# Weight low halves on GpSimd, row maxima scaled by a per-partition scalar

## The chip, the cores and the metric

The kernel runs on one core of a Trainium2 chip. The metric is the device time of one launch in microseconds (us). The engines are called by the profile's names: PE is TensorE (matmul), DVE is VectorE, ACT is ScalarE, POOL is GpSimd, and SP is SyncE, which here only issues DMAs. Each engine runs its own list of instructions in order and waits on semaphores for the others.

## The reference

Two blocks of two layers each, over 512 positions of width 1024, all in float32. The first block's layer projects x, runs four attentions (MLA, stick-breaking, Fox with forget gates, and one over a memory), gates each with a Silu, merges them with sigmoid gates, projects out and normalizes:

```python
    h = x @ w_in
    (c_q, c_kv, k_rope, sb_qkv, fox_qkv, fox_f, mem_q, gate_z, merge_r) = _split_last(h, IN_SPLITS)
    ...
    branches = (y_mla, y_sb, y_fox, y_mem)
    gate_z = gate_z.reshape(b, s, N_BRANCHES, BRANCH_WIDTH)
    merge_g = jax.nn.sigmoid(merge_r @ w_merge_up).reshape(b, s, N_BRANCHES, D_MODEL)
    merged = jnp.zeros_like(x)
    for n in range(N_BRANCHES):
        yb = branches[n].reshape(b, s, BRANCH_WIDTH) * jax.nn.silu(gate_z[:, :, n])
        merged = merged + merge_g[:, :, n] * (yb @ w_branch[n])
    out = merged @ w_out
    return _layer_norm(DEEPNORM_ALPHA * x + out, ln_g, ln_b)
```

The second block's layer has the same outline with other attentions: dense (a), a window with a sink (b), a neighbourhood with a table of biases (c), and differential attention (d), in which the softmax of one half of the channels is subtracted, times a factor, from that of the other half. Its branches are gated by Silu too, projected out, added to x, and RMS-normalized.

## The kernel before

Every float32 matmul is done as three products of halves. A number a is split into a high half ah, which PE's fast float32 format holds exactly, and a low half al = a − ah; `mm3` (L324) then adds ah·bh (L328), ah·bl (L329) and al·bh (L330) in PSUM. `split` (L317) makes the halves in two instructions: ACT copies the source into the high half, rounding it (L319), and DVE subtracts it from the source (L322). Activations are split so, from PSUM (tiles th and tl, zth and ztl), and weights too.

The weights lie in HBM as 184 units of 128 x 1024 numbers, 512 KB each, in the order of use. `w_prefetch` (L356) takes them in this order: a DMA on SP's queue brings a unit into one of three raw buffers (L376), and `split` makes wh and wl of it, in one of three pairs of buffers. The 28 units of the output projections (wo, wo2) go into an own pair of tiles (wout), and four units of the memory projection (m) are split in two halves each. `w_get` (L389) hands a unit out and lets the prefetch run up to three units ahead. A raw buffer is free again when the subtraction has read it.

`proj_fm` multiplies a unit with the layer's input. `softmax` (L515) takes the row maxima of a score tile on DVE, negated (L525 with a mask, L528 without), scales them where the scores carry a factor (L532: 64 instructions on 128 x 1 numbers, 32 in the MLA attention and 32 in the dense one), and gives them to ACT as the bias of Exp (L534). Transposes of p on PE follow (L552, tile T, split into th and tl), and the product with V (L564, L565, tile O). `silu` (L603) applies Silu to the gates on ACT (L608) and then loads the table of functions with Exp and Ln again (L611); ACT needs a table load wherever the function changes between the two sets. At the differential attention the scores are made at L1395 and combined at L1403.

`merge` (L1085) runs over eight output tiles m. A unit mu serves two of them, a unit wb one. For each branch, projmu gives the sigmoid gate, projwb the branch's product, and DVE adds them up (L1106, L1110). `w_out` (L1116) then takes all wo units, and for each quarter of the rows loads the residual y (L1126) on SP's queue and adds the product to it (L1134).

Attentions, gates and projections of a layer are written as generators, which two strings, ORDER1 and ORDER2, weave together. The final place of each instruction in its engine's list is set by a list scheduler, from its own estimates of durations, so an instruction that moves to another engine can shift others around it on all engines. POOL has almost nothing to do: it sets constants, the Fox rows (L1056, L1057) and the tiles V (L443) to fixed values.

Of the kernel before, what the change touches and what calls it, by code (L numbers as in the profile page):

```python
# [14 lines left out]
ALU = mybir.AluOpType  # L15
# [273 lines left out]
def cols(i, n=128):  # L289
    return slice(n * i, n * i + n)  # L290
# [11 lines left out]
WP = 3  # L302
# [8 lines left out]
class Build:  # L311
# [2 lines left out]
        self.layers = range(n_layers) if isinstance(n_layers, int) else n_layers  # L314


    def split(self, h, l, src, eng=None):  # L317
        if eng is None:
            self.nc.scalar.copy(h, src)  # L319
        else:  # L320
            eng.tensor_copy(h, src)
        self.nc.vector.tensor_tensor(l, src, h, ALU.subtract)  # L322

    def mm3(self, ps, pairs):  # L324

# [31 lines left out]
    def w_prefetch(self, upto):  # L357
        nc = self.nc
        while self.w_done < min(upto, len(UNITS)):
            i = self.w_done  # L360
            key = UNITS[i]
            wd = WIDTH.get(key[0], 1024)
            if key[0] in ("wo", "wo2"):
                if self.wout is None:
                    break
                parts = [tuple(w[:, key[2]] for w in self.wout)]
            elif key[0] == "m":
                if self.stp is None:
                    break
                parts = [(self.st("mh"), self.st("ml")) for _ in range(2)]  # L370
            else:
                parts = [tuple(self.wp.tile([128, 1024], F32R, tag=t, name=t)[:, :wd] for t in ("wh", "wl"))]
            raw = self.rawp.tile([128, 1024], F32, tag="raw", name="raw")
            n = 2 if i == 0 else 1
            for c in (cols(j, wd // n) for j in range(n)):
                nc.sync.dma_start(raw[:, c], self.ins["w"][i, :, c])  # L376
                if key[0] != "m":
                    self.split(*(t[:, c] for t in parts[0]), raw[:, c])
            if key[0] == "m":
                for j, (h, l) in enumerate(parts):  # L380
                    self.split(h, l, raw[:, cols(j, 512)])
            self.w_ready[key] = parts if key[0] == "m" else parts[0]
            self.w_done += 1
# [132 lines left out]
    def softmax(self, i, s, w, sm, mask=None, sscale=None, p=None, nm=None, top=BIG):  # L516


        nc = self.nc
        if p is None:  # L520
            p = self.pp.tile([128, w], F32, tag=f"p{i}", name="p", bufs=self.pb[i])
        nm = self.small(1, "nm") if nm is None else nm
        src, sc = s, 1.0
        if mask is not None:
            nc.vector.tensor_tensor_reduce(p[:, :w], s, mask, -1.0, top, ALU.add, ALU.min, nm)  # L525
            src, sc = p[:, :w], -1.0
        else:
            nc.vector.tensor_reduce(nm, s, AX.X, ALU.max, negate=True)  # L528
        if sscale is not None:
            sc = sscale[1 if mask is not None else 0]  # L530
            nm2 = self.small(1, "nm2")
            nc.vector.tensor_tensor(nm2, nm, sscale[0], ALU.mult)  # L532
            nm = nm2
        nc.scalar.activation(p[:, :w], src, AF.Exp, bias=nm, scale=sc, accum_out=sm)  # L534
        return p
# [945 lines left out]
```

## Time and profile before

| quantity | value |
|---|---|
| time, median of 3 runs | 1417.88 us (1415.82 to 1418.38) |
| the profiled execution | 1419.11 us, its span 1417.3 us |
| mean granted PE clock, as a share of full speed | 0.986 |
| PE busy | 1363.2 us, 7112 matmuls |
| DVE busy | 999.9 us, 2077 instructions |
| ACT busy | 832.3 us, 1672 instructions |
| POOL busy | 4.3 us, 12 instructions |

The span is what the trace covers, from the first instruction to the last. Busy times of engines overlap, so they don't add up to it. The chain is the sequence of work that ended last, followed back from the end: at each step to what released it, or to the instruction before it on its engine. The granted clock is what the chip allowed PE to run at in a stretch, 1.00 being full speed.

### The profile page before, as it was taken

How to read it: one execution, taken by the hardware profiler on the slowest of the kernel's cores; microseconds unless marked ns; L12 is line 12 of the kernel's file. 1: busy time of each engine (PE TensorE's matmuls, PEld its weight loads, DVE VectorE, ACT ScalarE, POOL GpSimd, SP SyncE). 2: the span in 40 equal slices, each digit the busy share in tenths (PEclk: the TensorE clock that was granted, in tenths of full speed). 3: DMA queues.
4: the chain of work that ended last, by engine and by line, in shares of the span. 5: the costliest groups of instructions: out<-in, count | busy, mean ns of one | idle time of the engine just before them, and what ended most of it. 6: DMA issues, size and time to landing. Idle time of an engine off the chain costs nothing.

```text
span 1417.3 us, 20005 instructions
## 1 busy us (share of the span) xinstructions
PE 1363.2 (96%) x7112; PEld 1111.0 (78%) x7112; DVE 999.9 (71%) x2077; ACT 832.3 (59%) x1672; POOL 4.3 (0%) x12
## 2 busy tenths in 40 slices
PE   8999998999999999998999999999999999999998
PEld 7887786777789777877777788877777888877776
DVE  6666545898764776257989675887777575886785
ACT  5584547765413765476856243776866346667763
POOL 0000000000000000000000000000000000000000
PEclk9999999999999999999999999999999999999999
DMA  7534222213625424222135436323434265215241
GB/s 238 172 105 118 72 75 80 75 60 108 207 100 159 139 71 117 75 81 80 41 89 179 163 115 180 111 60 103 131 100 145 109 177 150 75 45 151 62 140 67
DMA packets 61266, 160.31 MB, mean 113 GB/s; under 512 B 11056, under 2 KB 11696, under 8 KB 61168
## 3 DMA queue, kind: packets, MB, share of 16 engines
q1 hardware_dynamic: 61168, 159.05, 37.8%
q8 instruction: 56, 0.92, 0.3%
q14 instruction: 42, 0.34, 0.1%
HBM read 117.92 MB, written 8.91 MB: 89 GB/s over the span
## 4 chain that ended last, share of the span: by engine, by line
PE 77%; ACT 8%; DVE 8%; DMA 4%; issue 2%; SPq 0%; DVEq 0%; ACTq 0%
PE proj L328 11%; PE proj L329 11%; PE proj L330 11%; PE T L552 3%; PE pso L328 3%; PE pso L329 3%; PE pso L330 3%; PE O L564 3%; PE O L565 2%; PE s L901 2%; PE projv L329 2%; PE projv L330 2%; PE projv L328 2%; PE projwb L329 2%; PE projwb L330 2%
## 5 line engine op out<-in xcount | busy, mean ns | idle before, releaser
L328 PE MATMUL proj<-zth,wh 128*128 128x512 f32 (+1 forms) x864 | 323.9, 375 | 9.5 <-ACT wh L319 5.8
L329 PE MATMUL proj<-ztl,wh 128*128 128x512 f32 (+1 forms) x864 | 323.4, 374 | 0.3
L330 PE MATMUL proj<-zth,wl 128*128 128x512 f32 (+1 forms) x864 | 322.9, 374 | 0.0
L322 DVE TENSOR_TENSOR wl<-raw,wh 128x1024 fp32r<-128x1024 f32 (+2 forms) x153 | 183.1, 1197 | 135.1 <-ACT wh L319 126.7
L319 ACT CAST wh<-raw 128x1024 fp32r<-128x1024 f32 (+2 forms) x153 | 157.6, 1030 | 170.4 <-PE proj L329 139.7
L328 PEld LDWEIGHTS proj<-zth,wh 128*128 128x128 f32 x864 | 164.1, 190 | 32.9 <-ACT wh L319 5.8
L330 PEld LDWEIGHTS proj<-zth,wl 128*128 128x128 f32 x864 | 164.2, 190 | 23.7 <-DVE wl L322 1.0
L329 PEld LDWEIGHTS proj<-ztl,wh 128*128 128x128 f32 x864 | 164.3, 190 | 22.8 <-DVE ztl L322 0.7
L322 DVE TENSOR_TENSOR tl<-T,th 128x512 fp32r<-128x512 f32 (+3 forms) x176 | 98.9, 576 | 28.3 <-ACT th L319 27.7
L552 PE MATMUL T<-ct,p 128*128 128x128 f32 x560 | 103.6, 279 | 9.9 <-ACT p L534 7.7
L319 ACT CAST th<-T 128x512 fp32r<-128x512 f32 (+3 forms) x176 | 85.5, 498 | 41.8 <-PE T L552 39.0
L552 PEld LDWEIGHTS T<-ct,p 128*128 128x128 f32 x560 | 71.1, 142 | 30.5 <-ACT p L534 11.3
L528 DVE TENSOR_REDUCE nm<-s 128x1 f32<-128x512 f32 (+1 forms) x128 | 77.5, 616 | 19.6 <-PE s L513 10.2
L534 ACT ACTIVATE p<-s,nm 128x512 f32<-128x512 f32 (+1 forms) x96 | 59.1, 619 | 17.3 <-DVE nm L528 16.7
L564 PE MATMUL O<-th,V 128*128 128x512 f32 (+3 forms) x176 | 62.4, 371 | 2.6 <-ACT th L319 2.2
L565 PE MATMUL O<-tl,V 128*128 128x512 f32 (+3 forms) x160 | 59.3, 376 | 5.0 <-DVE tl L322 4.8
L328 PE MATMUL pso<-wout,zth 128*128 128x512 f32 x128 | 51.7, 404 | 4.7 <-DVE y L1134 4.7
L328 PE MATMUL projv<-wh,zth 128*128 128x256 f32 (+1 forms) x192 | 55.0, 287 | 0.0
L330 PE MATMUL projv<-wh,ztl 128*128 128x256 f32 (+1 forms) x192 | 54.7, 285 | 0.0
L329 PE MATMUL projv<-wl,zth 128*128 128x256 f32 (+1 forms) x192 | 54.6, 284 | 0.0
L330 PE MATMUL projwb<-y,wl 128*128 128x512 f32 x128 | 51.6, 403 | 0.0
L328 PE MATMUL projwb<-y,wh 128*128 128x512 f32 x128 | 51.1, 399 | 0.2
(380 smaller groups left out, 2927.7 us busy)
## 6 DMA issues: line engine op xcount, KB each, us to landing
raw<-in_w_dram SPq DMA_DIRECT2D x173, 512.0 KB
xs<-y SPq DMA_DIRECT2D x12, 512.0 KB
ks<-hs SPq DMA_DIRECT2D x32, 128.0 KB
early<-xs SPq DMA_DIRECT2D x16, 256.0 KB
bias<-in_bias_dram SPq DMA_DIRECT2D x8, 448.0 KB
qs<-hs SPq DMA_DIRECT2D x24, 128.0 KB
qs<-ls SPq DMA_DIRECT2D x24, 128.0 KB
hs<-ls SPq DMA_DIRECT2D x24, 128.0 KB
```

The source lines that it names most:

```text
L319: self.nc.scalar.copy(h, src)
L322: self.nc.vector.tensor_tensor(l, src, h, ALU.subtract)
L328: self.nc.tensor.matmul(ps, ah, bh, start=i == 0, stop=False)
L329: self.nc.tensor.matmul(ps, ah, bl, start=False, stop=False)
L330: self.nc.tensor.matmul(ps, al, bh, start=False, stop=i == n - 1)
L528: nc.vector.tensor_reduce(nm, s, AX.X, ALU.max, negate=True)
L534: nc.scalar.activation(p[:, :w], src, AF.Exp, bias=nm, scale=sc, accum_out=sm)
L552: nc.tensor.transpose(T[:, cols(a)], P[i][:, c : c + 128], self.ident)
L564: nc.tensor.matmul(o[:, c], vsel(j), th[:, c], start=j == 0, stop=False)
L565: nc.tensor.matmul(o, vsel(j), tl[:, :w], start=False, stop=j == nk - 1)
L901: nc.tensor.matmul(z[:, c:w], m, x, start=False, stop=n == len(sums) - 1, skip_group_check=True)
```

## The change

`split` gets a parameter for the engine that does the subtraction. `w_prefetch` passes POOL for all units from the fourth on, except the four m units: 177 of 181 subtractions of weight halves other than those of the m units, 139 of 1024 columns, six of 876, two of 768, two of 384, and the 28 of wo and wo2. The scaling of the row maxima becomes a tensor_scalar whose scalar comes from a 128 x 1 tile.

```diff
-    def split(self, h, l, src, eng=None):
+    def split(self, h, l, src, eng=None, sub=None):
         if eng is None:
             self.nc.scalar.copy(h, src)
         else:
             eng.tensor_copy(h, src)
-        self.nc.vector.tensor_tensor(l, src, h, ALU.subtract)
+        (sub or self.nc.vector).tensor_tensor(l, src, h, ALU.subtract)
...
                 if key[0] != "m":
-                    self.split(*(t[:, c] for t in parts[0]), raw[:, c])
+                    self.split(*(t[:, c] for t in parts[0]), raw[:, c], sub=nc.gpsimd if i >= WP else None)
...
             nm2 = self.small(1, "nm2")
-            nc.vector.tensor_tensor(nm2, nm, sscale[0], ALU.mult)
+            nc.vector.tensor_scalar(nm2, nm, sscale[0], None, ALU.mult)
             nm = nm2
```

The scheduler places much else anew. ACT's list at the first group of Silus in layer 2, before (L534 is Exp; th, ot and V are copies out of PSUM):

```order
L608 ACT_TABLE_LOAD
L608 ACTIVATE z<-z 128x512
L319 CAST th<-T 128x512
L608 ACTIVATE z<-z 128x512
L319 CAST th<-T 128x512
L608 ACTIVATE z<-z 128x512 x2
L611 ACT_TABLE_LOAD
L592 COPY ot<-O 64x512
L534 ACTIVATE p_9115,s_9113<-s,nm 128x512
```

And the beginning of the same group after the change:

```order
L608 ACT_TABLE_LOAD
L608 ACTIVATE z<-z 128x512
L592 COPY ot<-O 64x512
L534 ACT_TABLE_LOAD
L534 ACTIVATE p,sums<-s,nm 128x512
L534 ACTIVATE p_9115,s_9113<-s,nm 128x512
L608 ACT_TABLE_LOAD
L608 ACTIVATE z<-z 128x512
L534 ACT_TABLE_LOAD
L534 ACTIVATE p,sums<-s,nm 128x512
L534 ACTIVATE p_9132,s_9130<-s,nm 128x512
L414 CAST V<-projv 128x4x64
```

The group of four Silus with two table loads has become one with nine loads up to its last, with Exps in between, and layer 3 has the same. The groups of layers 0 and 1 have five loads instead of seven each.

PE's list in a merge, at the turn from one mu unit (wh_2627, wl_2628) to the next (wh_3250, wl_3251), before; wh_3317 and wl_3318 are the wb unit that is fetched there:

```order
L329 MATMUL projwb_3373<-y_3206,wh_3244 128x512
L328 MATMUL projmu_3367<-mr_3240,wh_2627 128x512
L329 MATMUL projmu_3367<-mr_3241,wh_2627 128x512
L330 MATMUL projmu_3367<-mr_3240,wl_2628 128x512
L330 MATMUL projwb_3373<-y_3205,wl_3245 128x512
L328 MATMUL projwb_3402<-y_3177,wh_3317 128x512
L329 MATMUL projwb_3402<-y_3178,wh_3317 128x512
L328 MATMUL projmu_3396<-mr_3240,wh_3250 128x512
L329 MATMUL projmu_3396<-mr_3241,wh_3250 128x512
L330 MATMUL projmu_3396<-mr_3240,wl_3251 128x512
L330 MATMUL projwb_3402<-y_3177,wl_3318 128x512
```

After:

```order
L330 MATMUL projmu_3367<-mr_3240,wl_2628 128x512
L329 MATMUL projwb_3373<-y_3202,wh_3244 128x512
L330 MATMUL projwb_3373<-y_3201,wl_3245 128x512
L328 MATMUL projwb_3373<-y_3205,wh_3244 128x512
L329 MATMUL projwb_3373<-y_3206,wh_3244 128x512
L330 MATMUL projwb_3373<-y_3205,wl_3245 128x512
L328 MATMUL projmu_3396<-mr_3240,wh_3250 128x512
L329 MATMUL projmu_3396<-mr_3241,wh_3250 128x512
L330 MATMUL projmu_3396<-mr_3240,wl_3251 128x512
L328 MATMUL projwb_3402<-y_3177,wh_3317 128x512
L329 MATMUL projwb_3402<-y_3178,wh_3317 128x512
L330 MATMUL projwb_3402<-y_3177,wl_3318 128x512
```

Before, the high half's products of the new wb unit stand ahead of the new mu unit's; after, they stand behind them, directly ahead of the low half's. From the matmul that is the last to read the buffer which the wb unit takes over, to the one that reads its low half, there are ten matmuls before and twelve after.

## Rows read from the trace of the kernel before

**Rows 1.** The page: span, busy time by engine, chain by engine.

```profile
span 1417.3 us, 20005 instructions
...
PE 1363.2 (96%) x7112; PEld 1111.0 (78%) x7112; DVE 999.9 (71%) x2077; ACT 832.3 (59%) x1672; POOL 4.3 (0%) x12
...
PE 77%; ACT 8%; DVE 8%; DMA 4%; issue 2%; SPq 0%; DVEq 0%; ACTq 0%
```

**Rows 2.** Windows: stretch, us, busy PE, PEld, DVE, ACT, POOL, clock, DMA, GB/s.

```profile
200.00:250.00 50.00, 45.08 (x218) 35.76 (x217) 29.59 (x72) 34.96 (x67) 0.00 (x0) 0.93 0.26 72
875.00:925.00 50.00, 49.99 (x277) 41.80 (x276) 33.64 (x65) 32.71 (x65) 0.00 (x0) 1.00 0.45 126
899.90:917.90 18.00, 18.00 (x125) 16.16 (x124) 13.66 (x31) 15.60 (x32) 0.00 (x0) 1.00 0.27 76
```

**Rows 3.** DVE's groups by form, weight subtractions: busy us, mean ns, idle before.

```profile
L322 DVE TENSOR_TENSOR wl<-raw,wh 128x1024 fp32r<-128x1024 f32 x141 | 172.3, 1222 | 122.0 <-ACT wh L319 113.6 <-DMA bias<-in_bias_dram 2.4 <-PE s L512 2.0
...
L322 DVE TENSOR_TENSOR wout<-raw,wout 128x1024 fp32r<-128x1024 f32 x28 | 34.2, 1222 | 5.1 <-ACT wout L319 5.1
...
L322 DVE TENSOR_TENSOR wl<-raw,wh 128x876 fp32r<-128x876 f32 x6 | 6.4, 1071 | 12.8 <-ACT wh L319 12.8
```

**Rows 4.** Waits: who waits for whom, total us, times, longest.

```profile
DVE wl L322 <- ACT wh L319: 126.7, 61, 7.2
```

**Rows 5.** Chain that ended last, in order of time: start, us, piece.

```profile
60.77 0.59 DVE wl L322
...
249.75 1.08 DVE wl L322
250.83 0.73 DVE rw L748
...
345.52 1.23 DVE wout L322
...
346.77 3.61 DMA raw<-in_w_dram
...
1286.21 1.24 DVE wl L322
```

**Rows 6.** Timeline of POOL, a memset: start, us, instruction, idle before.

```profile
64.93 0.53 POOL L1056 MEMSET cqrows<- 128x512 f32 x1 [64.49 <-DMA raw<-in_w_dram]
```

**Rows 7.** Timeline at the turn of a mu unit in layer 0's merge.

```profile
310.33 1.05 ACT L319 CAST wh<-raw 128x1024 fp32r<-128x1024 f32 x1 [0.24 <-PE projwb L329]
...
311.42 1.23 DVE L322 TENSOR_TENSOR wl<-raw,wh 128x1024 fp32r<-128x1024 f32 x1
...
312.74 0.46 PE L330 MATMUL projwb<-y,wl 128*128 128x512 f32 x1
```

**Rows 8.** Timeline at the end of layer 0: SP's queue and DVE.

```profile
340.45 31.13 SPq L376 DMA_DIRECT2D raw<-in_w_dram  x13
...
372.76 1.13 SPq L1126 DMA_DIRECT2D y<-in_x_dram  x2
...
381.23 1.28 DVE L1134 SCALAR_TENSOR_TENSOR y<-y,pso 128x512 f32<-128x512 f32 x2 [7.84 <-DMA y<-in_x_dram]
```

**Rows 9.** DVE's groups by form: scaling of maxima, tensor_scalar, the merge's sums.

```profile
L1110 DVE TENSOR_TENSOR sg<-sg 128x512 f32<-128x512 f32 x48 | 33.0, 688 | 0.5
...
L532 DVE TENSOR_TENSOR nm<-nm,qsc 128x1 f32<-128x1 f32 x64 | 9.7, 151 | 0.5
...
L1157 DVE TENSOR_SCALAR ssv<-ss,ssv 128x1 f32<-128x1 f32 x13 | 2.8, 212 | 0.8 <-ACT junk L1154 0.4
```

**Rows 10.** ACT's groups: the table loads around Silu.

```profile
L608 ACT ACT_TABLE_LOAD x14 | 18.0, 1283 | 0.2
...
L611 ACT ACT_TABLE_LOAD x10 | 12.8, 1283 | 0.2
```

**Rows 11.** Timeline of ACT in layer 2, first Silu load to last Exp.

```profile
899.99 1.28 ACT L608 ACT_TABLE_LOAD   x1
...
917.16 0.69 ACT L534 ACTIVATE p<-s,nm 128x512 f32<-128x512 f32 x1 [0.41 <-DVE nm L528]
```

## The prediction

> **What bounds the kernel now.** I read the page's busy times first: PE works 96% of the span, DVE 71%, ACT 59%, and POOL 4.3 us in all; of the chain that ended last 77% is PE and only 8% DVE and 8% ACT [rows 1]. So the work that the change takes from DVE is nearly all hidden, and what can be won or lost is the time in which PE stands still or runs at a low clock. The windows say where that is: from 200 to 250 us PE is busy 45.1 of 50 us at a mean granted clock of 0.93, while from 875 to 925 us it is busy throughout at 1.00, 277 matmuls, 0.18 us each [rows 2]. In a stretch of the first kind a faster DVE can help, and in one of the second kind every delay of an engine that feeds PE is new.
>
> **What DVE gives away.** Per launch 177 subtractions leave DVE: 139 of 1024 columns at 1.222 us, six of 876 at 1.071, 28 for wo and wo2 at 1.222, and four narrower ones of under 1.07 us. That is 169.9 + 6.4 + 34.2 = 210.5, some 213 us with the four [rows 3]. DVE also stands before these instructions for 126.7 us until the ACT cast is done [rows 4]; as an engine runs its list in order, all DVE work queued behind such a wait gets free of it. What of it is on the path that sets the end? The chain shows steps like the one at 249.75 us, where a weight subtraction of 1.08 us stands ahead of the DVE step for which PE goes on to wait, and this is relief when moved; and steps like the one at 345.52 us, where a DMA into a raw buffer starts only once the subtraction has released it, and this becomes worse when the subtraction gets slower [rows 5]. The chain has 24 such pieces of together 23 us, from the one at 60.77 to the one at 1286.21 us [rows 5], about half of them of the first kind. Bounds: 0 (POOL takes DVE's place on the chain) to −14 us (twelve pieces of 1.2 us). I take a little more than the middle, since the 126.7 us of waiting go as well: **−8**.
>
> **What a subtraction costs on POOL.** The trace of before has no POOL arithmetic; the nearest row is a memset of 128x512 in 0.53 us [rows 6]. A pass over 1024 columns is then about 1.0 us, and a subtraction has one pass to write and two to read: between 1.0 and 3.0 us, and I take 2.0, an estimate for reading the two operands. 177 of them are some 350 us, a quarter of the span, so POOL can't be the bound by its sum; what counts is that each low half is ready about 0.8 us later than with DVE's 1.22.
>
> The Trainium skill has a price, in "GPSIMD Engine Reference", section 3.1: its table gives a two-operand fp32 operation of 2048 columns 4497 ns on GpSimd and 2293 on VectorE. By that ratio of 1.96 an estimate here is 2.4 us, and the two terms below that go by it (merge and layer ends) would be some 3 us larger together; no run here shows it yet.
>
> **Where the 0.8 us is seen.** For most units nothing waits: PE reads the high half first, and the unit is fetched three units ahead. At the merge it is different: before the turn from one mu unit to the next the wl of the wb unit is done at 312.65 us and its first reader on PE starts at 312.74 [rows 7]. There are three such places in each of the two merges, six in all. In the new order PE has twelve matmuls instead of ten between the release of the buffer and the matmul that needs the low half; two more at 0.18 us cover about 0.4 of the 0.8 us. **+0.5** each, **+3** in all; bounds 0 (a price of 1.6 us or less) and +8 (3.0 us, less the same cover: six times 1.4). At the ends of layers 0 and 1 the loads of y stand on SP's queue behind 13 loads of raw buffers, each waiting for a subtraction to release its buffer, and DVE's y step then waits 7.84 us for them [rows 8]. Four or so subtractions in a row lie there one behind the other through three raw buffers; 0.8 us later on each, less what ACT's 1.05 us cast hides: **+2** each, **+4** for two; bounds 0 and +8. Also queued behind POOL's subtractions, in order, are its memsets of the Fox rows and of V; they stood there before with nothing else around [rows 6], and I see no consumer near: 0.
>
> **The other edit.** 64 row maxima are scaled with a tensor_tensor of 151 ns; the nearest tensor_scalar that takes a second operand from a tile has 212 ns [rows 9]. If that is the price, DVE gets 64 × 0.06 = 3.9 us longer and Exp starts 0.06 us later each time. DVE has some 213 us more of free time, so this costs **0**, bounds −1 and +1.
>
> **What the changed order does.** The scheduler places everything anew, since it takes the subtractions for later or earlier than before. The costliest effect that I find is on ACT. In layer 2 before, the four Silus stood together between two table loads. In the new order the four are torn apart, with Exps between them, and each change of function needs a load: nine loads where there were two, and the same in layer 3. In layers 0 and 1 the group has five instead of seven. In all the order has 51 loads instead of 41, at 1.283 us each [rows 10]. Layers 2 and 3 get 7 × 1.283 = 9.0 us more on ACT each, in the very stretch where PE has no gap. From the first load at 899.9 us to the end of the last Exp at 917.9 us ACT is busy for 15.6 of 18.0 us and PE for all of them [rows 2, 11], so 2.4 us of the 9.0 go into its idle time and the last Exp comes some 6.6 us later. Does PE wait for it? The p that these Exps make goes to the transposes of the same attention, and the projections that PE has at that time stand in its list between them: they cover some at the beginning, and then PE stands. I take **+6** each, **+12** for both layers; bounds 0 (PE has projections to do until then, and they are not missing later) and +18 (all of it). In layers 0 and 1 the stretches are of the other kind, PE has gaps there already and the clock granted is down to 0.93 in the mean [rows 2]: two loads less, 2.6 us of ACT, are worth **−2** each, **−4**; bounds −5 and 0.
>
> **Sum.** −8 + 3 + 4 + 0 + 12 − 4 = +7. The profiled execution took 1419.11 us, 1.2 us above the median of 1417.88, and 1.8 of it lie outside its span; the terms are differences, so they are put on the median: **1425 us**.
>
> **Rivals.** *Faster:* PE covers the loads in layers 2 and 3 and the relief on DVE is at its full bound: −14 + 3 + 4 + 0 − 4 = −11, **1407 us**. For it speaks that DVE's 126.7 us of waiting go with the 213 us of work [rows 3, 4], and that PE has other work in every stage; against it that 77% of the chain are PE itself, and that the loads fall where PE has no gap. Chance 0.30.
>
> *Nothing to measure:* relief 8, the loads half covered (+6), +7 for merge and layer ends, less 4: +1, within 3 us of 1418. Speaks for it that PE's own work fixes 96% of the span. Chance 0.17.
>
> *Slower by more: DVE and POOL hold each other up.* Both read SBUF. If a subtraction on POOL keeps DVE from working in the meantime, or the other way round, DVE gets no relief, and the low halves come later by what DVE works at that moment. Part of DVE's work reads two tiles in SBUF, 33.0 us of it in the merge's sums alone [rows 9]. Then the relief is 0, and each of the 24 chain pieces is longer by 0.8 us, +19 in place of the terms for merge and layer ends: 19 + 12 − 4 = +27, **1445 us**. It decides when a subtraction that overlaps such DVE work takes over 2.8 us, or the DVE rows grow by over a tenth. Nothing in the trace of before speaks for or against it, since POOL is never busy there beside DVE. Chance 0.13.
>
> [...]
>
> *The change doesn't do what it says:* the subtractions could run on POOL one behind the other with DVE idle, so that nothing overlaps. POOL's list has only memsets beside them, so I give this no chance of its own.
>
> **How the numbers follow.** Forecast 0.40, faster 0.30, nothing 0.17, locked 0.13. The measurement of this kernel can tell about 0.2%, 2.8 us. Faster is 0.30, same 0.17 plus a little of the forecast's lower side, 0.19, slower 0.51. The range goes from 1403 (the faster rival and 4 us for a cheap subtraction at the merges and layer ends) to 1441 (the forecast with loads, merge and layer ends each at their upper bound, +6 + 5 + 4 = +15, and a microsecond): it leaves out the locked case and a larger gain.
>
> **What the changed profile would show.** Right: DVE's busy time down by about 210 us, POOL's at 300 to 430; 51 table loads; PE waits for ACT's p in the layers 2 and 3 after the Silus, of 4 to 8 us each, in the stretch without gaps; at the mu turns waits for POOL of half a microsecond. Wrong: a POOL subtraction at 1.5 us or below (merge and layer ends cost nothing), or at 3 and above with DVE's rows longer (the lock); PE busy throughout behind the torn Silus (the table loads are hidden, and the faster rival holds); or PE's idle time in 200 to 300 us down by more than 10 us.

## The result and the profile after

The changed kernel takes **1522.28 us** (median of 4, 1520.83 to 1523.11) against 1417.09 us for the kernel before beside it: 1.0736 times as long, 95% interval 1.0716 to 1.0755. It is slower by 105 us, where 7 were forecast. Its page, in the parts of [rows 1]:

```profile
span 1520.6 us, 20117 instructions
...
PE 1390.1 (91%) x7112; PEld 1124.2 (74%) x7112; DVE 950.5 (63%) x1900; ACT 843.0 (55%) x1682; POOL 435.9 (29%) x189
...
PE 35%; DVE 11%; ACT 8%; issue 3%; POOL 1%; DMA 1%; SPq 1%; ACTq 0%; DVEq 0%; POOLq 0%
```

Two numbers of the busy line don't fit. DVE gave away 213 us of work and is only 49 us less busy, so some 160 us have come to what it kept. (Busy time counts it once when two instructions overlap. Summed instruction by instruction, what DVE kept is 132 us longer.) And PE does the same 7112 matmuls in 27 us more, at a mean granted clock of 0.970 in place of 0.986. (The chain of this profile breaks off more often than that of before, its shares add up to 60%, so I don't read it.)

The groups of DVE and POOL by form show where DVE's time has gone. Columns as in [rows 3]: busy us, mean ns, idle before.

```profile
L322 DVE TENSOR_TENSOR tl<-T,th 128x512 fp32r<-128x512 f32 x96 | 65.1, 687 | 40.6 <-ACT th L319 40.4
...
L1110 DVE TENSOR_TENSOR sg<-sg 128x512 f32<-128x512 f32 x48 | 59.0, 1230 | 1.4
L1106 DVE TENSOR_TENSOR sg<-projwb,sg 128x512 f32<-128x512 f32 x64 | 43.6, 687 | 31.4 <-PE projwb L330 19.4 <-ACT sg L1103 8.8 <-ACT zth L319 2.8
...
L1403 DVE SCALAR_TENSOR_TENSOR p<-p,rl,p 128x512 f32<-128x512 f32 x32 | 31.3, 978 | 0.1
...
L322 DVE TENSOR_TENSOR ztl<-sg,zth 128x512 fp32r<-128x512 f32 x16 | 24.9, 1559 | 4.3 <-ACT zth L319 4.1
...
L532 DVE TENSOR_SCALAR nm<-nm,qsc 128x1 f32<-128x1 f32 x64 | 13.4, 210 | 1.3
```

```profile
L322 POOL TENSOR_TENSOR wl<-raw,wh 128x1024 fp32r<-128x1024 f32 x139 | 341.4, 2462 | 898.3 <-ACT wh L319 771.4 <-PE s L513 39.5 <-ACT mt L873 21.1
L322 POOL TENSOR_TENSOR wout<-raw,wout 128x1024 fp32r<-128x1024 f32 x28 | 72.3, 2609 | 87.4 <-ACT wout L319 87.3
```

SBUF holds the kernel's tiles, and PSUM takes PE's sums. L1110 reads two tiles in SBUF and went from 688 [rows 9] to 1230 ns; L1106, the line before it in the code and of the same size, reads one of its two inputs from PSUM and stays at 687. The same pair are ztl<-sg,zth (1559 ns; both in SBUF) and tl<-T,th (687; T in PSUM). The timeline shows one instance. Start, us, instruction, the DVE rows first and then POOL's:

```profile
332.15 3.46 DVE L1110 TENSOR_TENSOR sg<-sg 128x512 f32<-128x512 f32 x2
335.54 0.68 DVE L1106 TENSOR_TENSOR sg<-projwb,sg 128x512 f32<-128x512 f32 x1
```

```profile
332.55 5.33 POOL L322 TENSOR_TENSOR wl<-raw,wh 128x1024 fp32r<-128x1024 f32 x2 [3.66 <-ACT wh L319]
```

The two sums of L1110 would take 1.4 us and take 3.46: the second stands until the first of POOL's two subtractions is over. L1106 then runs beside the second subtraction in its usual 0.68 us. A small instruction is held as long as a large one. L351 multiplies 128 x 8 numbers, which takes 0.17 us elsewhere:

```profile
651.23 0.17 DVE L350 TENSOR_TENSOR rs_t<-rs_y 128x8 f32<-128x8 f32 x1
651.43 2.25 DVE L351 TENSOR_TENSOR rs_t<-rs_t,v 128x8 f32<-128x8 f32 x1
```

```profile
648.91 4.75 POOL L322 TENSOR_TENSOR wl<-raw,wh 128x1024 fp32r<-128x1024 f32 x2 [7.38 <-ACT wh L319]
```

I compared every DVE instruction with the median of its form in the kernel before. 99 of them are longer by over 0.1 us and overlap a subtraction on POOL; they are longer by 1.3 us in the mean and 133 us together. (Four more, of L632, are 1.5 us longer together, overlap nothing on POOL and are as long in the kernel before; they are left out of all counts of held instructions here.) Those held read two tiles in SBUF, or are copies, casts and tensor_scalars with an immediate operand, which run at about twice the rate (some 0.42 us for 512 columns). What reads PSUM, what reduces, and the tensor_scalars of one column with a scalar from a tile are not held; of L532, 18 of 64 overlap a subtraction, and none is longer by more than 2 ns than the median of its row.

PE pays for it. Summed over all rows, its waits for DVE go from 24 to 67 us, for ACT from 17 to 29, for POOL from 0 to 23: 77 us more of standing. With the 27 us at a lower clock that is the 104 us. The largest of these rows (who waits for whom, us, times, longest):

```profile
PE s L901 <- DVE sp L321: 14.4, 10, 4.4
PE projwb L330 <- POOL wl L322: 11.0, 6, 3.5
PE rep L620 <- DVE hrep L617: 9.0, 6, 3.8
PE pso L329 <- POOL wout L322: 7.1, 4, 1.8
```

### The profile page after: what moved, and what is told of

It reads as the page before. It is cut to its first block, busy times and chain, and to the rows that moved or that the text cites. A ratio compares the mean times of both kernels' runs of the same rounds, so it can differ in the third digit from the quotient of the medians.

```text
span 1520.6 us, 20117 instructions
## 1 busy us (share of the span) xinstructions
PE 1390.1 (91%) x7112; PEld 1124.2 (74%) x7112; DVE 950.5 (63%) x1900; ACT 843.0 (55%) x1682; POOL 435.9 (29%) x189
## 4 chain that ended last, share of the span: by engine, by line
PE 35%; DVE 11%; ACT 8%; issue 3%; POOL 1%; DMA 1%; SPq 1%; ACTq 0%; DVEq 0%; POOLq 0%
PE proj L328 5%; PE proj L329 5%; PE proj L330 5%; PE T L552 2%; ACT p L534 2%; PE pso L329 2%; PE pso L330 2%; PE pso L328 2%; PE O L564 1%; PE O L565 1%; ACT wh L319 1%; PE O L587 1%; DVE tl L322 1%; PE s L512 1%; PE s L513 1%
## 5 line engine op out<-in xcount | busy, mean ns | idle before, releaser
L322 POOL TENSOR_TENSOR wl<-raw,wh 128x1024 fp32r<-128x1024 f32 (+2 forms) x149 | 359.6, 2419 | 947.4 <-ACT wh L319 820.4
L328 PE MATMUL proj<-zth,wh 128*128 128x512 f32 (+1 forms) x864 | 327.2, 379 | 8.7 <-ACT wh L319 5.6
L330 PE MATMUL proj<-zth,wl 128*128 128x512 f32 (+1 forms) x864 | 327.0, 379 | 2.3 <-POOL wl L322 2.3
L329 PE MATMUL proj<-ztl,wh 128*128 128x512 f32 (+1 forms) x864 | 327.3, 379 | 0.3
L319 ACT CAST wh<-raw 128x1024 fp32r<-128x1024 f32 (+2 forms) x153 | 157.5, 1030 | 165.1 <-issue 83.0
L552 PE MATMUL T<-ct,p 128*128 128x128 f32 x560 | 107.3, 281 | 9.5 <-DVE p L1403 6.5
L322 POOL TENSOR_TENSOR wout<-raw,wout 128x1024 fp32r<-128x1024 f32 x28 | 72.3, 2609 | 87.4 <-ACT wout L319 87.3
L534 ACT ACTIVATE p<-s,nm 128x512 f32<-128x512 f32 (+1 forms) x96 | 59.0, 618 | 14.0 <-DVE nm L528 13.2
L1106 DVE TENSOR_TENSOR sg<-projwb,sg 128x512 f32<-128x512 f32 x64 | 43.6, 687 | 31.4 <-PE projwb L330 19.4
L1110 DVE TENSOR_TENSOR sg<-sg 128x512 f32<-128x512 f32 x48 | 59.0, 1230 | 1.4
```

The lines of the kernel that those rows point to most:

```text
L322: (sub or self.nc.vector).tensor_tensor(l, src, h, ALU.subtract)
L328: self.nc.tensor.matmul(ps, ah, bh, start=i == 0, stop=False)
L329: self.nc.tensor.matmul(ps, ah, bl, start=False, stop=False)
L330: self.nc.tensor.matmul(ps, al, bh, start=False, stop=i == n - 1)
L552: nc.tensor.transpose(T[:, cols(a)], P[i][:, c : c + 128], self.ident)
L1106: nc.vector.tensor_tensor(sg, pb, sg, ALU.mult)
```

## Theories

My theory from these rows is **exclusion**: a subtraction on POOL and a DVE instruction of the kinds named keep each other out of SBUF, each until the other ends. The rivals: **lateness**, that the low halves are ready over a microsecond later and raw buffers come free later; and **order**, that the ten more table loads and the rest of the scheduler's moves cost the time, DVE's longer rows being beside the point.

## Experiments

Each was timed against the kernel before in three rounds; kernels that ran together share its runs, whose median lay between 1417.3 and 1420.6 us.

| run | what | us | against before (95%) |
|---|---|---|---|
| fill_for_sub | POOL fills twice instead of subtracting | 1434.23 | 1.008 to 1.013 |
| sub_aside | before, POOL subtracts constants beside it | 1542.29 | 1.082 to 1.091 |
| maxima_only | only the edit of L532 | 1408.78 | 0.991 to 0.996 |
| halves_only | only the edit of the low halves | 1542.66 | 1.084 to 1.089 |
| every_other_unit | half of the units on POOL | 1478.96 | 1.038 to 1.044 |
| aside_fill | before, POOL fills beside it | 1429.39 | 1.005 to 1.010 |
| fill_once | as fill_for_sub, one fill | 1428.58 | 1.005 to 1.010 |
| fill_three | as fill_for_sub, three fills | 1448.18 | 1.018 to 1.024 |
| four_pieces | subtractions in four pieces | 1519.98 | 1.069 to 1.074 |
| aside_pieces | sub_aside in four pieces, untied | 1630.85 | 1.149 to 1.153 |
| aside_paced | sub_aside in four pieces, tied | 1473.85 | 1.035 to 1.042 |
| fill_silu_whole | fill_for_sub, Silus kept together | 1459.89 | 1.026 to 1.031 |
| after_silu_whole | the changed kernel, Silus together | 1528.56 | 1.074 to 1.081 |
| maxima_silu_whole | maxima_only, Silus together | 1423.36 | 1.001 to 1.004 |

### POOL without reading

```diff
-        (sub or self.nc.vector).tensor_tensor(l, src, h, ALU.subtract)
+        if sub is None:
+            self.nc.vector.tensor_tensor(l, src, h, ALU.subtract)
+            return
+        n = l.shape[1]
+        sub.tensor_tensor(l[:, :8], src[:, :8], h[:, :8], ALU.subtract)
+        for _ in range(2):
+            sub.memset(l[:, 8 : n - 8].bitcast(F32), 0.0)
+        sub.tensor_tensor(l[:, n - 8 :], src[:, n - 8 :], h[:, n - 8 :], ALU.subtract)
```

> As the changed kernel, but the subtraction on POOL is replaced by two subtractions of 8 columns (first and last, so that it still waits for the cast and holds the raw buffer to its end) and two fills of the columns between, about 2 us that read nothing; the weights' low halves are left out by that. It has the 51 table loads and nearly the order of the changed kernel. Theory (POOL's reading of SBUF and DVE's two-input work exclude each other): DVE's sums of the merge (L1110 before) go back from 1.23 to 0.69 us, and the time falls to 1425 to 1440 us, what is left being the table loads and the later low halves. Rival 1 (the low halves and raw buffers come too late): 1505 to 1520. Rival 2 (the new order, with ten more table loads): 1505 to 1520, with DVE's rows back at 0.69 all the same.

This kernel leaves the weights' low halves out, but for 16 columns of each unit; PE does the same 7112 matmuls at a mean granted clock of 0.986, as before. 1434.23 us: 88 of the 105 us are gone, and DVE's sum is back where it was (its line is L1117 here):

```profile
L1117 DVE TENSOR_TENSOR sg<-sg 128x512 f32<-128x512 f32 x48 | 33.2, 691 | 1.4
```

The kernel keeps all 51 table loads and nearly the changed order on every engine, and POOL is as long at a unit (by its rows 0.95 us a fill and 0.22 a short subtraction, 2.3 in all). So neither order nor lateness is where the bulk went. What remains against the kernel before, some 14 us, is left to them and to 17 DVE instructions, copies, casts and tensor_scalars, that are still held in this run, by 9.5 us together.

### The lock by itself

```diff
-        (sub or self.nc.vector).tensor_tensor(l, src, h, ALU.subtract)
+        if sub is not None:
+            sub.tensor_tensor(self.dump[:, :8], h[:, :8].bitcast(F32), self.ct[:, :8], ALU.subtract)
+            sub.tensor_tensor(self.dump, self.ct[:, :1024], self.ct[:, :1024], ALU.subtract)
+        self.nc.vector.tensor_tensor(l, src, h, ALU.subtract)
```

> The kernel before, with the same order on PE, DVE, ACT and SP, and all subtractions on DVE as before; beside them POOL does 177 subtractions of 128x1024 constants into a tile that nobody reads, each after the cast of its unit. Theory (exclusion): DVE's rows of two SBUF inputs grow, those that read PSUM don't, and the time rises by 80 to 180 us, to 1500 to 1600, although nobody waits for a result of POOL. Rivals 1 and 2 (late low halves, order): within 5 us of 1417.

The rest of this edit makes the tile dump and puts L532 back as it was before. 1542.29 us, 122 more than before, with the order of PE, DVE, ACT and SP word for word that of before and no consumer of POOL's result. DVE's groups, as in [rows 3]:

```profile
L325 DVE TENSOR_TENSOR wl<-raw,wh 128x1024 fp32r<-128x1024 f32 x141 | 225.4, 1599 | 115.2 <-ACT wh L319 108.4 <-PE s L515 1.8 <-PE s L1399 1.2
...
L325 DVE TENSOR_TENSOR tl<-T,th 128x512 fp32r<-128x512 f32 x96 | 64.7, 685 | 18.0 <-ACT th L319 17.6
...
L325 DVE TENSOR_TENSOR wout<-raw,wout 128x1024 fp32r<-128x1024 f32 x28 | 52.9, 1899 | 0.0
```

Here the weight subtractions are on DVE, read two tiles in SBUF, and are among the held: 1599 and 1899 ns for 1222. In all 133 instructions are held, by 163 us, which goes with the run being even slower than the changed kernel. With this and the run before it, exclusion is shown from both sides: without POOL's long reads most of the loss goes, and with POOL's subtractions as the only addition it is there.

The control has the same kernel with two fills in place of POOL's large subtraction:

```diff
-            sub.tensor_tensor(self.dump, self.ct[:, :1024], self.ct[:, :1024], ALU.subtract)
+            sub.memset(self.dump, 0.0)
+            sub.memset(self.dump, 0.0)
```

> As the run with POOL's subtractions aside, in the same order (that of the kernel before), but POOL fills the unread tile twice, some 2 us, in place of the subtraction; only 8 columns of each unit are read by it. Theory (exclusion needs POOL to read SBUF): 1417 to 1425, no DVE group longer than before by over a few per cent. If any POOL work holds DVE up: near 1540 as with the subtractions.

1429.39 us, a little above what I expected, and the trace shows what is still held. The instructions with two SBUF inputs are free now (69 instructions of five such groups start while a fill is running, and none is longer by over 0.1 us). Two of these groups, as in [rows 3]:

```profile
L326 DVE TENSOR_TENSOR wl<-raw,wh 128x1024 fp32r<-128x1024 f32 x141 | 172.1, 1221 | 122.0 <-ACT wh L319 115.3 <-PE s L516 1.8 <-PE s L333 1.5
...
L1115 DVE TENSOR_TENSOR sg<-sg 128x512 f32<-128x512 f32 x48 | 33.0, 687 | 0.5
```

But copies and casts are still held, until a fill ends. Timeline, DVE's row and POOL's:

```profile
616.45 1.25 DVE L621 COPY hrep<-sums 128x512 f32<-128x512 f32 x1
```

```profile
615.28 0.95 POOL L324 MEMSET dump<- 128x1024 f32 x1
616.29 1.13 POOL L325 MEMSET dump<- 128x1024 f32 x1
```

The copy takes 1.25 us (0.42 before), until POOL's second fill is through at 617.42 and the copy itself is done. 39 DVE instructions are held so, 19 us together, 35 of them copies, casts and tensor_scalars with immediates. A tensor_scalar of 512 columns with a scalar from a tile (L1165) is among them too, with 1.21 us for 0.49. So my "needs POOL to read SBUF" was too narrow: POOL's subtractions hold the two-input work, and its fills hold the work at double rate as well. POOL is busy for 33% of this run, more than in the changed kernel, and the granted clock is 0.986 as before, so POOL's being busy does not by itself lower the clock.

### The two edits apart

maxima_only has the line of L532 and nothing else of the change, halves_only all the rest:

```diff
-            nc.vector.tensor_tensor(nm2, nm, sscale[0], ALU.mult)
+            nc.vector.tensor_scalar(nm2, nm, sscale[0], None, ALU.mult)
```

> The kernel before with the second edit alone, the scaling of the row maxima by a per-partition scalar. All theories: L532 at 210 ns as in the changed kernel, 3.8 us of DVE, hidden; 1415 to 1422 us, the spread being what the scheduler's moves do.

> The changed kernel with the scaling of the maxima as before, a tensor_tensor of two tiles in SBUF. Theory (exclusion): 64 more DVE instructions that can be held, of which the share that meets a subtraction is held for 1 to 2 us each, on the way to Exp: 1522 to 1545 us, and L532 with a mean over 300 ns. Rivals: 1518 to 1524, as the changed kernel less the 3.8 us of DVE at most.

The maxima alone: **1408.78 us**, 0.7% faster than before and better than I expected; the low halves alone: 1542.66. L532, first in halves_only, where it is a tensor_tensor, then in maxima_only:

```profile
L532 DVE TENSOR_TENSOR nm<-nm,qsc 128x1 f32<-128x1 f32 x64 | 23.9, 373 | 0.8
```

```profile
L532 DVE TENSOR_SCALAR nm<-nm,qsc 128x1 f32<-128x1 f32 x64 | 13.1, 204 | 0.6
```

Beside POOL the tensor_tensor of two SBUF tiles is held (8 of 64, by 1.8 us in the mean), and its hold falls between row maximum and Exp; the tensor_scalar, one column with its second operand as a scalar from a tile, is never held in the changed kernel. So in the changed kernel the second edit is worth some 20 us, part of which can be the order. Without POOL it costs 53 ns more an instruction, and the kernel is some 10 us faster all the same. The scheduler had moved much for it (over 800 lines of difference in PE's list), but I ran nothing that keeps the order and changes the instruction, so the cause of these 10 us stays open.

### How the loss grows

```diff
-sub=nc.gpsimd if i >= WP else None
+sub=nc.gpsimd if i >= WP and i % 2 else None
```

> The changed kernel with every second unit's subtraction on POOL and the others on DVE (88 or so of 177 moved). Theory (exclusion): each subtraction on POOL holds DVE by itself, and those left on DVE read two tiles in SBUF and can be held as well: half of the 88 us between 1434 and 1522 or a little more, 1460 to 1485. If the loss came only where two follow closely, it would be under a quarter: below 1450.

1478.96 us. 55 DVE instructions are held by 67 us together, half of the 133, and 61 of the 105 us are lost. With half of the subtractions a little over half of the loss is there; smaller shares were not run.

```diff
-        (sub or self.nc.vector).tensor_tensor(l, src, h, ALU.subtract)
+        n = l.shape[1] // (4 if sub else 1)
+        for j in range(4 if sub else 1):
+            c = cols(j, n)
+            (sub or self.nc.vector).tensor_tensor(l[:, c], src[:, c], h[:, c], ALU.subtract)
```

> The changed kernel, in its order, with each subtraction on POOL cut into four of a quarter of the columns. By the changed kernel's trace (1.008 us for 384 columns, 2.40 for 1024) a piece of 256 takes some 0.73 us and the four 2.9, so the low halves are complete 0.5 us later than in one piece. Theory (exclusion, one instruction at a time): a DVE instruction that comes meanwhile waits for the end of one piece, at most 0.7 us in place of 2.4, and the 88 us of the lock fall to between 30 and 50: 1460 to 1490. If POOL keeps DVE out from its first piece to its last, or lateness is what costs: 1520 to 1540.

1519.98 us: my expectation was wrong. The holding that the trace shows halved, to 71 us on 156 instructions, and next to nothing was gained. Was holding not the price after all, or did the lateness eat it up, since four pieces of 256 columns take 2.9 us from first to last at the median and up to 4.2? Two more runs were to tell. The first had four pieces of 256 columns in sub_aside, the second three fills in fill_for_sub:

```diff
-            sub.tensor_tensor(self.dump, self.ct[:, :1024], self.ct[:, :1024], ALU.subtract)
+            for j in range(4):
+                c = cols(j, 256)
+                sub.tensor_tensor(self.dump[:, c], self.ct[:, c], self.ct[:, c], ALU.subtract)
...
-        for _ in range(2):
+        for _ in range(3):
             sub.memset(l[:, 8 : n - 8].bitcast(F32), 0.0)
```

> As the run with POOL's subtractions aside (1542 us), in the same order, but each cut into four of 256 columns; nobody waits for a result, so being late costs nothing here. If a DVE instruction is held until the end of one POOL instruction only (theory): DVE's rows grow by a half or less of the 162 us there, and the time falls to 1455 to 1490. If what counts is how long POOL reads in all, or what DVE keeps POOL from: 1530 to 1550.

> As the run with two fills (1434 us), with three, some 3.3 us from the first piece to the last, as late as the four pieces of the run before; nothing but 16 columns of each unit is read, and low halves are left out. If being late by 0.9 us more than in the changed kernel eats up what shorter holds gain there: 1460 or more. If lateness costs little: 1434 to 1446.

aside_pieces failed as an experiment: only the first piece was tied to its unit, so the others ran ahead in long trains. It took 1630.85 us, and 209 of the 212 us by which its span is longer had arisen when layer 0's output projection began. What it does show is what a train does. Timeline, DVE and then POOL:

```profile
59.91 30.32 DVE L327 TENSOR_TENSOR wl<-raw,wh 128x1024 fp32r<-128x1024 f32 x2 [1.12 <-ACT wh L319]
```

```profile
54.57 19.48 POOL L326 TENSOR_TENSOR dump<-ct 128x256 f32<-128x256 f32 x34
74.00 0.22 POOL L323 TENSOR_TENSOR dump<-wh,ct 128x8 f32<-128x8 f32 x1
74.16 9.19 POOL L326 TENSOR_TENSOR dump<-ct 128x256 f32<-128x256 f32 x16
```

One of the two subtractions of DVE was held for 27.5 us, through more than forty pieces that followed each other, none of which let it in. In four_pieces this happens too: a DVE instruction at the end of layer 2, while eight pieces run:

```profile
1167.94 5.98 DVE L1158 TENSOR_TENSOR n<-y,rmsg 128x512 f32<-128x512 f32 x1
```

```profile
1167.68 5.69 POOL L325 TENSOR_TENSOR wl<-raw,wh 128x256 fp32r<-128x256 f32 x8
```

fill_three, at 1448.18, lies between its two expectations and bounds what lateness costs: 14 us more than two fills for a microsecond more. Not all of it is lateness, since DVE's copies, casts and tensor_scalars are held by 28 us there, and by 9.5 with two fills. And with the pieces tied to their units, so that at most four follow each other:

```diff
-            sub.tensor_tensor(self.dump[:, :8], h[:, :8].bitcast(F32), self.ct[:, :8], ALU.subtract)
+            sub.tensor_tensor(self.dump.rearrange("p (a b) -> p a b", b=128)[:, :, 0], h[:, :8].bitcast(F32), self.ct[:, :8], ALU.subtract)
```

> As the run before with four pieces aside, but the short instruction that reads the unit's high half writes a column of every piece, so that the four pieces of a unit can't run before its cast; the order of the other engines is that of the kernel before. Compared with one piece aside (1542 us). If a DVE instruction is held to the end of one POOL instruction: 1455 to 1490, DVE's rows grown by half of the 162 us or less. If POOL's reading in all is what counts: 1530 to 1560.

1473.85 us where the whole subtractions took 1542.29, with 259 holds of 0.35 us in the mean in place of 133 of 1.2. So short POOL instructions do make the lock cheaper, to less than half, where nobody waits for their result. In four_pieces somebody does. Its parts compare so: up to the middle of layer 0's attentions it is 8 us ahead of the changed kernel, and at the end of that layer 4 behind. Over the whole kernel PE's waits for DVE are 15 us less than in the changed kernel (52 for 67), those for POOL 4 more (27 for 23) and those for ACT 2 more, and PE itself is busy 3 us longer at a granted clock of 0.966. Why the holding that was saved did not come back as time I did not take apart; by fill_three lateness can explain 14 us of it at most, and what held pieces and trains of pieces cost was not measured.

### Lateness

One, two and three fills differ by one fill of about 0.95 us a unit and little in order. They differ too in how long DVE's copies, casts and tensor_scalars are held: 6, 9.5 and 28 us.

```diff
-        for _ in range(2):
-            sub.memset(l[:, 8 : n - 8].bitcast(F32), 0.0)
+        sub.memset(l[:, 8 : n - 8].bitcast(F32), 0.0)
```

> As the run with two fills (1434 us), with one fill of about 1 us, so that the low halves are ready as early as with DVE's 1.22 us, in nearly the same order. Low halves are left out as there. If the lateness at the merges and layer ends costs what the prediction says (+3 and +4): 1425 to 1429. If it is the order alone: 1432 to 1436.

1428.58, 1434.23 and 1448.18 us: 6 us for the second microsecond, 14 for the third, with the longer holds in them. The waits of PE for the merge's low half, in the changed kernel 11.0 us at six places, are not in the rows of one fill, 0.4 us with two fills and 6.0 with three. So being late by itself is cheap at these places at POOL's real price of 2.4 us. What makes 11 of it in the changed kernel is not shown by a run of its own; there POOL is held by DVE in its turn (single subtractions take up to 2.88 us), and ACT and DVE are behind.

### The table loads

```diff
             es.enter_context(tc.issue_after(self.gate_copy.ins))
+            if self.last_exp is not None:
+                es.enter_context(tc.issue_after(self.last_exp))
...
-            nc.scalar.preload_act_table_set(EXPS)
+            self.pin = nc.scalar.preload_act_table_set(EXPS).ins
...
+            if self.pin is not None:
+                es.enter_context(self.tc.issue_after(self.pin))
+            self.last_exp = nc.scalar.activation(p[:, :w], src, AF.Exp, bias=nm, scale=sc, accum_out=sm).ins
```

> As the run with fills in place of POOL's subtractions, but the Silus of a group are kept together: the first of them may stand only behind the last Exp written before, and later Exps only behind the load that ends the group. 31 table loads instead of 51. Low halves are left out as there. If the torn Silus cost what the prediction says (+6 in each of the layers 2 and 3): 1418 to 1426 us, from 1434. If the loads are hidden: 1431 to 1437.

> The changed kernel with the Silus of a group kept together, 31 table loads instead of 51. Theory (exclusion): it does nothing to the lock, and the time stays at 1500 to 1522, lower than 1522 by the same 0 to 16 us as the run with fills. Rival 2 (order and loads): near 1430.

> All subtractions on DVE, the scaling of the maxima by a per-partition scalar (1409 us alone), and the Silus of a group kept together: 31 table loads instead of 41. If the loads in layers 0 and 1 cost what the prediction says (2 us for each two): 1400 to 1407. If they are hidden: 1406 to 1413.

All three went the other way: 26, 6 and 15 us slower than the same kernel in the scheduler's own order, although ACT has 31 loads in place of 51 (41 in maxima_only). To keep the Silus together, they wait for the last Exp written before, and later Exps wait for them; that makes over 1300 lines of difference in PE's list in the first pair, and the loss there is spread over the layers, so the runs don't isolate a load's price. They show that keeping the Silus together in this way costs more than the loads that it saves. The price itself is read from the changed kernel's trace, where the torn Silus of layer 2 and their loads lie between 970 and 996 us. PE's waits from 960 to 1030 us:

```profile
PE T L552 <- DVE p L1403: 3.2, 2, 1.8
PE s L1395 <- ACT p L534: 2.5, 3, 1.3
```

2.5 us for ACT's p, and the same in layer 3; the DVE wait beside it is the lock's (L1403 is one of the held).

## Why the prediction was wrong, by its own steps

**The case.** The direction was right and the size was off by a factor of 15, because the mechanism that decided stood third among the rivals, at 0.13 and 1445 us. Two steps failed. The first: the forecast's sum has no term for POOL's subtractions holding DVE up. It put that at nothing and took a relief of 8 us, and the range left the locked case out, for the reason that "nothing in the trace of before speaks for or against it", which is no reason for a low chance. The runs showed 88 of the 105 us in its place (1522.28 against 1434.23 us with fills). The Trainium skill states the exclusion in "SBUF — State Buffer", section "Who interferes with whom": a VectorE instruction with two SBUF inputs contends with a GpSimd instruction that reads SBUF, and not with one that only writes it; with at most one SBUF input it doesn't contend, unless it runs in one of the two-port modes, which copies, casts and tensor_scalars can enter. This case's traces agree on two-input work (L1110, 688 to 1230 ns beside subtractions, 687 beside fills), on PSUM inputs (L1106, 687 ns) and on double-rate copies (0.42 to 1.25 us beside a fill).

The second step that failed is the price of the locked rival: I priced it by the 24 chain pieces of [rows 5], 0.8 us each, as if only the moved instruction got later. What gets later is what DVE kept, 99 instructions by 1.3 us in the mean, a little over half of a POOL subtraction's 2.46 us. One sign was set wrong with it: the lock was to show in a POOL subtraction of 3 us and above, and the subtractions stayed at 2.46 in the mean while DVE's rows grew. How many instructions are held could not have been read from the trace of before by a simple product. In the changed kernel some 700 DVE instructions read two tiles in SBUF or are copies, casts or immediate tensor_scalars, and POOL is busy 29% of the span. 700 by 0.29 by half a subtraction is an estimate of 250 us of holding, nearly twice the 133 measured.

**POOL's price.** Taken 2.0 us, measured 2.46 in the mean and 2.40 at the median. The fill of [rows 6] was a poor neighbour. The ratio of 1.96 in the Trainium skill ("GPSIMD Engine Reference", section 3.1) was right: the estimate from it, 2.4 us, is the median here.

**DVE's relief, −8.** Not to be had. DVE lost 213 us of work and got 133 back as holding. Without POOL's long reads (fill_once, low halves about as early as on DVE) the kernel is still 10 us slower than before, so the relief is smaller than what the new order and the 6 us of holds that are left there cost; these are not told apart.

**Merge, +3, and layer ends, +4.** The mechanism is there with the lock, larger at the merges: 11.0 us at six places. At the layer ends DVE's wait for the loads of y at L1134 grew by 0.2 us in layer 0 (8.0, 7.8 before [rows 8]) and by 1.7 in layer 1 (10.5, 8.8 before), and PE no longer stands for that step (4.7 us before). But PE waits 7.1 us for wout's low halves, which I did not name. By the fills, a second microsecond of lateness costs 6 us at most, near the 7 us of the two terms; that is an agreement of size only, as the terms' places were not isolated.

**The maxima, 0.** The price per instruction was right (204 to 210 ns for the 212 of [rows 9]). That it would be faster alone, by 0.7%, I did not see, and why it is stays open.

**The table loads, +12 and −4.** 51 loads came, at 1283 ns each, but PE's wait for it is 2.5 us a layer, not 6: the step that failed is "then PE stands", since PE's own work covered more than half of the 6.6 us.

## What to carry to other kernels

Before work is moved from DVE to POOL, count what stays on DVE: instructions with two inputs in SBUF, and copies, casts and immediate tensor_scalars at double rate. Each of them that meets a POOL subtraction can wait for half of one or more, and small instructions on the path to PE are held as long as large ones. Their number, times POOL's busy share, times half a POOL instruction, came out nearly twice too high here, so it warns of the size and doesn't forecast it; a run like sub_aside, with POOL's work beside the old kernel, shows the lock before anything is moved. What reads PSUM, reduces, or scales a single column by a per-partition scalar was free of it here. Short POOL instructions hold for less, unless they follow each other in a train.

The fastest kernel of this study is the one with the second edit alone, 1408.78 us (0.991 to 0.996 of before).

## What the runs showed that I had not expected

- Back-to-back POOL instructions can keep DVE out through all of them: one DVE subtraction stood for 27.5 us, while others got in between two pieces after 0.4 us.
- Fills on POOL, which read nothing, leave two-input work alone (687 ns for L1110's sum) and hold copies and casts: 0.42 to 1.25 us.
- The holding is mutual: an instruction of 128 x 8 numbers on POOL takes 0.2 us alone, and 0.86 us in the mean in sub_aside, where DVE's own subtraction of the unit starts at the same moment.
- An edit of 0.05 us an instruction, with the new order that the scheduler made for it, moved the time by some 10 us, and the constraint that keeps the Silus together by up to 26: more than most single terms of the sum.
